# Low halves of weight pieces by accumulating DMAs in state space, attention and around the norms, with a new order in attention

## The chip, the cores and the metric

The program runs on one core of one Trainium2 chip. The metric is the device time of one execution in microseconds; the time before is the median of three runs. Engines: PE (TensorE, matmuls), DVE (VectorE), ACT (ScalarE), POOL (GpSimd) and SP (SyncE, which here issues most DMAs).

## The reference

A decoder trunk of two layers over 512 tokens of width 1024. Layer 0 mixes with a short convolution and a state space (S5), layer 1 with sparse attention: an indexer with 8 heads scores all earlier keys, the best 128 keys of each query are kept, and attention runs over those. Cut to what matters:

```python
def swiglu(x, w1, w3, w2):
    return (jax.nn.silu(x @ w1) * (x @ w3)) @ w2

def dsa_mixer(proj, cos_a, sin_a, cos_i, sin_i):      # layer 1
    q, k, v, qi, ki, wi = jnp.split(proj, C_SPLITS, axis=-1)
    ...                                                # rotary on q, k, qi, ki
        logits = jax.nn.relu(jnp.einsum('bthd,bsd->bths', qib.astype(f32), ki))
        score = jnp.einsum('bths,bth->bts', logits, wb)
        _, idx = lax.top_k(score, topk)                # topk = 128
    ...                                                # softmax(q k) v over the chosen keys

for i in range(DEPTH):                                 # DEPTH = 2
    h = layer_norm(DN_ALPHA * h + 0.5 * swiglu(h, ffn_w1[i, 0], ...), ln_g[i, 0], ln_b[i, 0])
    mix = ...                                          # layer 0: convolution and S5; layer 1: dsa_mixer
    h = layer_norm(DN_ALPHA * h + mix, ln_g[i, 1], ln_b[i, 1])
    h = layer_norm(DN_ALPHA * h + 0.5 * swiglu(h, ffn_w1[i, 1], ...), ln_g[i, 2], ln_b[i, 2])
    h = h + (p[i] @ ple_w_proj[i]) * jax.nn.sigmoid(h @ ple_w_gate[i])
```

There are six norms; below they are ln0 to ln5 in order of time.

## The kernel before

All data is f32, but a matmul takes operands of a shorter type (`fp32r`), so each operand is cut in a high part and a low part, and every product is three matmuls, high by high, high by low and low by high. The 337 blocks of weights ("pieces", 128 x 1024 f32, 512 KB each) flow through `Stream`: SP loads a piece into `wraw` (three buffers), ACT casts it to `whi` (L77), and another engine forms `wlo = wraw - whi` (L78). That engine is DVE, except between L970 and L1201 (most of attention), where `lo_engine` makes it POOL. Split pieces wait in a ring of `RING` = 7. `free` frees a used piece and splits the next one at this point of the program (`ahead`); `split_to(n)` sets how many pieces may stand split and not yet freed.

The order of instructions on every engine is that of the Python code (`manual_schedule`), so a cut stands in ACT's, DVE's or POOL's queue where `free`, `take` or `split_to` is called. Small work beside the matmuls is placed by a clock that counts matmul time (`tick`, `at`).

The stages: feed forward (L376), `tail` (L426), mixer, `tail`, feed forward, `tail`, `embed` (L1220), twice. `tail` is the end of a product with the norm woven into it: its last four pieces are multiplied for one quarter of the tokens after another, and each quarter is transposed, normalized and transposed back meanwhile. At its start the ring is filled to seven (the four pieces of the tail and three of the next stage); when three quarters of the tokens are through, `split_to(6)` splits one more, the fourth piece of the next stage. What follows a tail is a `group` (L284): four pieces, output columns in two halves of 256 tokens; in the first half (`h=0`) it needs all four pieces within 32 matmuls of 120 ns. At `h=1` it splits further ahead. After ln2 and ln5 `embed` follows instead.

The state space (`mixer_ab`, L730) is written as a row of `states(f)` and `output(f)` of four groups of channels, with products for the convolution (`hc`, `gc`, `gb`) between them. In one such round PE makes D from the inputs, DVE runs a scan (L796 to L816: `m`, `zz`, `hz`), and PE turns `hz` to outputs. `vv` is the gated convolution (L849 to L858), `L319` casts it to its high part `xh`, and the output product of L260 takes `xh`.

Attention (`mixer_dsa`, L939) makes index queries `qi` (four tiles), then the index key `ki`, with a rotary turn of each (`turn`: four DVE or POOL instructions), values `vs` (`values_in`), index weights `wi` (`weights_in`), and for each of the query tiles 1 to 3 scores: `index(i)` is eight index heads, each a matmul (L991), a relu on ACT (L994) and a multiply-add on DVE into `bias` (L996, L998). `choose(n, tiles)` runs n rounds of top-8 search on DVE (L1008 MAX8, L1010 MATCH_REPLACE8); a tile needs 16 rounds or fewer beyond the diagonal, here 16 for each of the tiles 1 to 3. Rounds that are left run inside the attention `step`s (`last_rounds`), and `chosen(i)` (L1062) turns what was found into a mask. A `step` is scores (L1102), a masked copy with maximum (L1105), an exponential (L1107), `normal` (L1109, scaling by L1114), a turn of the weights and the product with the values; heads of q and pieces of the output product (`project`) fill PE meanwhile.

Of the kernel before, what the change touches and what calls it, by code (L numbers as in the profile page):

```python
# [16 lines left out]
P = 128  # L17
T = 512
# [34 lines left out]
class Stream:  # L53
# [5 lines left out]
    def __init__(self, nc, ctx, tc, pieces):  # L59
        self.nc, self.pieces, self.n = nc, pieces, len(pieces)  # L60
        self.raw_pool = ctx.enter_context(tc.tile_pool(name="wraw", bufs=3))
        self.pool = ctx.enter_context(tc.tile_pool(name="wsplit", bufs=self.RING))
        self.raw, self.got = {}, {}
        self.loaded = self.split = self.used = self.freed = 0
        self.lo_engine = nc.vector

# [8 lines left out]

    def cut(self, t, hi, lo):
        self.nc.scalar.copy(hi, t)  # L77
        self.lo_engine.tensor_sub(lo, t, hi.bitcast(F))  # L78

    def _split(self):  # L80
        i = self.split
        while self.loaded <= i:
            self._load()
        self.got[i] = self.parts()
        self.cut(self.raw.pop(i), *self.got[i])
        self.split += 1
# [113 lines left out]
class Program:  # L200
# [73 lines left out]

    def whole(self):

        w = self.ws.take()
        b = self.bank("U")
        self.mm(b, w, self.x, range(KD), range(KD), slice(0, T))
        self.ws.free()  # L280
        self.lows()
        return b

    def group(self, done):  # L284
# [4 lines left out]
        for h in range(2):  # L289
            cols = slice(h * HALF, (h + 1) * HALF)  # L290
            if h:
                self.flush()
                ws.split_to(ws.RING - 1)
            for k0 in range(0, KD, 4):
                for m in range(0, 4, 2):
# [130 lines left out]
    def tail(self, g, g0, ln):  # L426
# [3 lines left out]
        w = [ws.take() for _ in range(4)]  # L430

        ws.split_to(ws.RING)
        ws.SPLIT = 4
# [296 lines left out]
    def mixer_ab(self, ln):  # L730
# [49 lines left out]
        self.group(have_u)  # L780
        self.pending = False

        def states(f):
# [143 lines left out]

    def turn(self, x, adder=None):

        nc = self.nc  # L930
        sin, cos = self.rope[1]
        sh = self.work.tile([P, 2, T], F, name="sh", tag="t4")
        nc.vector.stream_shuffle(sh[:, 0], x, [r ^ 8 if r < 16 else r for r in range(32)])
        nc.vector.tensor_mul(sh[:, 0], sh[:, 0], sin)
        adder = adder or nc.gpsimd
        adder.tensor_mul(sh[:, 1], x, cos)
        adder.tensor_add(x, sh[:, 0], sh[:, 1])

    def mixer_dsa(self, ln):  # L939
# [16 lines left out]

        def have(dst, b):
            nc.scalar.copy(dst, b)
            self.turn(dst)

        self.group(lambda m, b: [have(qi[:, m + i], b[i]) for i in range(2)])
        self.pending = False

        b = self.whole()
        for i in range(2):
            nc.scalar.copy(ki[64 * i:64 * i + 64], b[:64])
        wt = self.work.tile([8, T], F, name="wt", tag="t4")
        nc.scalar.activation(wt, b[64:72], AF.Copy, scale=WI_SCALE)
        self.turn(ki, v)
        ws.lo_engine = nc.gpsimd  # L970

# [11 lines left out]

        def index(i):

            n = (i + 1) * P
            sc = bias[i]
            for h in range(8):
# [8 lines left out]
                else:  # L997
                    v.scalar_tensor_tensor(sc, r[:, :n], wi[:, i, h:h + 1], sc, op0=OP.mult, op1=OP.add)  # L998
            nc.gpsimd.affine_select(sc[:, i * P:], sc[:, i * P:], pattern=[[-1, P]], compare_op=OP.is_ge,
                                    fill=NEG, base=0, channel_multiplier=1)  # L1000
# [46 lines left out]
        weights_in()  # L1047
        index(1)
        choose(6, (1,))
        values_in((2, 3))  # L1050
        ws.free(2)
        index(2)
        choose(2, (1, 2))
        run(head(k[:, 0], 0, "k"))
        index(3)
        choose(2, (1, 2))
        run(head(k[:, 1], 1, "k"))
        turn_heads([k[:, g] for g in range(2)], "k")
        choose(2, (1, 2))

        def chosen(i):
            v.tensor_scalar(bias[i], bias[i], -3.2e38, FAR, op0=OP.is_gt, op1=OP.mult)  # L1062

        for h, more in enumerate(((2, (1, 2)), (2, (1, 2)), (3, (2, 3)), (2, (2, 3)))):
            run(head(q[:, h], h, 0))
# [43 lines left out]
        def normal(i, g, r0):  # L1109
            pt, _, s = pr[i, g]  # L1110
            v.reciprocal(s[:, r0:r0 + 2], s[:, r0:r0 + 2])
            for r in (r0, r0 + 1):
                x = pt[:, r, :(i + 1) * P]
                v.tensor_scalar(x, x, s[:, r:r + 1], None, op0=OP.mult)  # L1114

# [64 lines left out]
        def last_rounds():  # L1180
            for i in range(11):
                choose(1, (3,) if i else (2, 3))
                if i in (0, 10):
                    chosen(3 if i else 2)
                yield
# [4 lines left out]
        filler = project(0)  # L1190
        step((2, 0), (1, 0), (0, 0, 0, 0, 3), (0, 0, 0, 0, 1), turn=True)
        step((0, 1), (2, 0), (2, 2, 0, 2, 3), (0, 1, 1, 0, 0))
        step((1, 1), (0, 1), (4, 2, 2, 1, 2), (0, 1, 0, 0, 0))
        step((2, 1), (1, 1), (1, 3, 1, 0, 0), (0, 1, 0, 0, 0))
# [4 lines left out]
        for _ in filler:  # L1199
            pass  # L1200
        ws.lo_engine = v  # L1201
        self.tail(O, 4, ln)
# [17 lines left out]
    def embed(self, last):  # L1220
# [12 lines left out]
        self.pending = False  # L1233
        ws.split_to(ws.RING - 1)
        new = None if last else self.pair()
        banks = self.first_two(4)
# [87 lines left out]
def pieces_dsa(w_in, w_out):  # L1324
# [3 lines left out]
    key[:, :72] = w_in[:, 2048:2120]  # L1328
    out = tiles_of(w_in[:, 1536:2048]) + tiles_of(key)
    out += [rows(w_in[:512, 1280:1536]), rows(w_in[512:, 1280:1536])]  # L1330
# [92 lines left out]
```

## Time and profile before

| | |
|---|---|
| time of 3 runs | 2010.99 us median, 2009.34 to 2012.37 |
| profiled execution | 2008.82 us, span 2006.5 us |
| PE | 1974.8 us busy, 98% of the span |
| DVE | 1048.9 us, 52% |
| ACT | 664.7 us, 33% |
| POOL | 113.6 us, 6% |
| DMA | 202.18 MB, mean 101 GB/s |

Rows of groups read: line, engine, operation, output and inputs by the program's names, count, then busy time and mean ns of one, then idle time of the engine before them and what ended it. Rows of the chain of waits: engine and line that waited, what released it, then us in all, how often, the longest or mean. Rows of the timeline: start in us, duration, engine, line, operation, and in brackets the idle time before it with its releaser. Stages of before by the timeline, in us: state space about 400 to 530, ln1's tail to 565 and then the group behind it, ln2 and embed about 944, attention about 1357 to 1550.

### The profile page before, as it was taken

Reading aid. Unit: us, or ns where it says so; the run is one execution under the profiler, and the core shown is the slowest. Engines: PE = TensorE matmul, PEld = TensorE weight load, DVE = VectorE, ACT = ScalarE, POOL = GpSimd, SP = SyncE. Lnnn points to the kernel's source line nnn. Section 1 sums busy time; section 2 is a strip of 40 time slices with the busy share of each in tenths; the row PEclk is TensorE's granted clock in tenths of the full one; section 3 lists DMA queues with packets and bytes.
Section 4 is the critical chain, followed back from the end, with each engine's and each line's share of the span. In section 5 each row is a group of like instructions: output and inputs, shape, how many; then the busy total and the mean of one; then the engine's idle time right before and its main releaser. Section 6 shows DMA issues by size and latency. Waiting matters only on the chain.

```text
span 2006.5 us, 23925 instructions
## 1 busy us (share of the span) xinstructions
PE 1974.8 (98%) x9550; PEld 1641.5 (82%) x9550; DVE 1048.9 (52%) x1959; ACT 664.7 (33%) x966; POOL 113.6 (6%) x120
## 2 busy tenths in 40 slices
PE   9999999998999999999999999998999999999999
PEld 7888888887798888888888888888776988888877
DVE  6457554667563333336555554357985643333363
ACT  5223333423353122225332222234443532222242
POOL 0001110011000000000000000002432000000000
PEclk9999999999999999999999999998999999999999
DMA  6333333344323232322332322312211142323312
GB/s 213 104 106 137 124 126 119 137 152 156 103 83 107 87 112 84 105 85 67 107 115 88 112 92 88 105 63 84 85 43 57 53 133 85 105 89 102 104 43 74
DMA packets 60559, 202.18 MB, mean 101 GB/s; under 512 B 7232, under 2 KB 11616, under 8 KB 59936
## 3 DMA queue, kind: packets, MB, share of 16 engines
q1 hardware_dynamic: 51840, 184.07, 27.8%
q0 software_dynamic: 4240, 14.44, 2.1%
q10 hardware_dynamic: 4368, 2.15, 0.4%
q8 instruction: 75, 1.23, 0.2%
q14 instruction: 36, 0.29, 0.0%
HBM read 189.10 MB, written 11.53 MB: 100 GB/s over the span
## 4 chain that ended last, share of the span: by engine, by line
PE 68%; DVE 3%; ACT 2%; issue 1%; POOL 0%; ACTq 0%; DVEq 0%; POOLq 0%
PE U L260 45%; PE D L260 14%; PE U L443 3%; PE D L443 2%; PE D L1133 1%; PE L L180 1%; PE U L1102 1%; PE U L143 0%; ACT whi L77 0%; PE D L143 0%; DVE pt L1114 0%; DVE wlo L78 0%; PE D L991 0%; PE U L273 0%; PE L L1124 0%
## 5 line engine op out<-in xcount | busy, mean ns | idle before, releaser
L260 PE MATMUL U<-xh,whi 128*128 128x512 f32 (+1 forms) x2000 | 749.0, 375 | 1.3 <-ACT xh L1139 1.0
L260 PE MATMUL U<-xl,whi 128*128 128x512 f32 (+1 forms) x2000 | 743.1, 372 | 2.1 <-DVE xl L1140 1.2
L260 PE MATMUL U<-xh,wlo 128*128 128x512 f32 (+1 forms) x2000 | 742.6, 371 | 0.0
L78 DVE TENSOR_TENSOR wlo<-wraw,whi 128x1024 fp32r<-128x1024 f32 (+1 forms) x321 | 393.8, 1232 | 307.8 <-ACT whi L77 306.9
L77 ACT CAST whi<-wraw 128x1024 fp32r<-128x1024 f32 (+1 forms) x337 | 350.5, 1045 | 550.4 <-PE D L260 295.9
L260 PEld LDWEIGHTS U<-xh,whi 128*128 128x128 f32 x2000 | 376.7, 188 | 71.2 <-ACT xh L1139 2.5
L260 PEld LDWEIGHTS U<-xl,whi 128*128 128x128 f32 x2000 | 376.7, 188 | 69.9 <-DVE xl L326 2.3
L260 PEld LDWEIGHTS U<-xh,wlo 128*128 128x128 f32 x2000 | 376.6, 188 | 64.5
L260 PE MATMUL D<-xh,whi 128*128 128x512 f32 x608 | 238.6, 392 | 8.2 <-ACT xh L319 7.7
L260 PE MATMUL D<-xl,whi 128*128 128x512 f32 x608 | 237.5, 391 | 0.0
L260 PE MATMUL D<-xh,wlo 128*128 128x512 f32 x608 | 237.2, 390 | 0.0
L373 DVE SCALAR_TENSOR_TENSOR gt<-gt,U 128x512 f32<-128x512 f32 x88 | 60.5, 687 | 264.5 <-PE U L260 208.3
L319 ACT CAST xh<-gt 128x512 fp32r<-128x512 f32 x88 | 54.6, 620 | 387.4 <-DVE gt L373 387.4
L260 PEld LDWEIGHTS D<-xh,whi 128*128 128x128 f32 x608 | 114.6, 188 | 34.6 <-ACT xh L319 8.1
L260 PEld LDWEIGHTS D<-xl,whi 128*128 128x128 f32 x608 | 114.6, 188 | 23.9 <-DVE xl L326 0.4
L260 PEld LDWEIGHTS D<-xh,wlo 128*128 128x128 f32 x608 | 114.6, 188 | 23.9
L424 DVE TENSOR_TENSOR u<-u,D 128x512 f32<-128x512 f32 x64 | 43.9, 687 | 112.7 <-PE D L260 112.7
L422 DVE SCALAR_TENSOR_TENSOR u<-u,D 128x512 f32<-128x512 f32 x40 | 27.4, 687 | 111.1 <-PE D L260 111.1
L326 DVE TENSOR_TENSOR xl<-gt,xh 128x512 fp32r<-128x512 f32 x88 | 60.3, 685 | 8.2 <-ACT xh L319 8.2
L372 ACT ACTIVATE gt<-U 128x512 f32<-128x512 f32 x88 | 52.0, 591 | 17.6 <-PE U L260 17.6
L186 DVE TENSOR_SCALAR u<-L,lnw 128x128 f32<-128x128 f32 x96 | 32.7, 403 | 26.0 <-PE L L180 26.0
L78 POOL TENSOR_TENSOR wlo<-wraw,whi 128x1024 fp32r<-128x1024 f32 x16 | 38.3, 2404 | 68.3 <-PE U L260 44.6
(318 smaller groups left out, 1553.3 us busy)
## 6 DMA issues: line engine op xcount, KB each, us to landing
wraw<-wts SPq DMA_DIRECT2D x333, 512.0 KB, 3.5
s5d<-big POOLq DMA_DIRECT2D x20, 256.0 KB, 5.1
u<-x SPq DMA_DIRECT2D x8, 256.0 KB, 5.5
s5d<-big POOLq DMA_DIRECT2D x4, 512.0 KB, 3.4
pin<-s5d SPq DMA_DIRECT2D x2, 1024.0 KB, 8.8
pin<-s5d POOLq DMA_DIRECT2D x2, 1024.0 KB, 5.3
out<-u SPq DMA_DIRECT2D x7, 256.0 KB, 2.0
pout<-s5d SPq DMA_DIRECT2D x2, 768.0 KB, 10.2
```

Of the source, the lines that this page charges most:

```text
L77: self.nc.scalar.copy(hi, t)
L78: self.lo_engine.tensor_sub(lo, t, hi.bitcast(F))
L180: p.nc.tensor.transpose(b[:, j * P:(j + 1) * P], self.z[:, c, j * P:(j + 1) * P], p.ident)
L186: p.nc.vector.tensor_scalar(out, x, gam, bet, op0=OP.mult, op1=OP.add)
L260: self.nc.tensor.matmul(out, lhsT=p[:, s], rhs=q[:, xk, cols], start=first and i == 0 and j == 0, stop=last and i == n - 1 and j == 2)
L319: self.nc.scalar.copy(hi[:, j, :], src)
L326: self.nc.vector.tensor_sub(out, src, hi)
L372: nc.scalar.activation(t[:, 0], pa, AF.Silu)
L373: nc.vector.scalar_tensor_tensor(t[:, 1], t[:, 0], 0.5, pb, op0=OP.mult, op1=OP.mult)
L422: self.nc.vector.scalar_tensor_tensor(u, u, ALPHA, d, op0=OP.mult, op1=OP.add)
L424: self.nc.vector.tensor_add(u, u, d)
L443: self.nc.tensor.matmul(b, lhsT=x, rhs=y, start=False, stop=k == TAIL - 1 and j == 2)
```

## The change

1. `cut` has a second way. When `by_dma` is set, ACT casts the high part as before (L79 after), ACT then writes the negative of the same rounded value into `wlo` (L81), and POOL issues a DMA that reads the piece from device memory a second time and adds it to `wlo` in place (L82). Else DVE subtracts as before (L84). `lo_engine` and its use of POOL are gone.
2. `by_dma` is set at the start of every `tail`, after the first `group` of the state space and after the first `group` of attention; it is cleared at `h=1` of the next `group` and in `embed`. 63 of the 337 pieces go this way: 28 around the six norms (4, 4, 6, 4, 4, 6), 35 within state space and attention. 47 DVE and 16 POOL subtractions go; 63 ACT multiplications and 63 POOL DMAs of 512 KB come.
3. Attention: the key's piece goes first; `turn` is all on DVE (two of its four instructions were POOL's for the four `qi`); both pairs of values come ahead of `index(1)`; a third of a head's projection follows every second index head; rounds of `choose` move: before the steps tile 2 gets 12 instead of 15 and tile 3 gets 2 instead of 5, in the steps `last_rounds` has 14 entries instead of 11, of which four (before: one) work on both tiles.
4. `normal`'s scaling goes from DVE (L1114) to ACT (L1140), 32 instructions.

The remarks behind # on lines of the diff name the function that the line stands in.

```diff
-    def cut(self, t, hi, lo):
+    def cut(self, t, hi, lo, piece=None):
         self.nc.scalar.copy(hi, t)
-        self.lo_engine.tensor_sub(lo, t, hi.bitcast(F))
+        if self.by_dma and piece is not None:
+            self.nc.scalar.mul(lo, t, -1.0)
+            self.nc.gpsimd.dma_start(lo, piece, accum_op=OP.add)
+        else:
+            self.nc.vector.tensor_sub(lo, t, hi.bitcast(F))
...
             if h:                                   # group
                 self.flush()
                 ws.split_to(ws.RING - 1)
+                ws.by_dma = False
...
+        ws.by_dma = True                            # tail
         ws.split_to(ws.RING)
...
         self.group(have_u)                          # mixer_ab
         self.pending = False
+        ws.by_dma = True
...
-    def turn(self, x, adder=None):
+    def turn(self, x):
...
-        adder = adder or nc.gpsimd
-        adder.tensor_mul(sh[:, 1], x, cos)
-        adder.tensor_add(x, sh[:, 0], sh[:, 1])
+        nc.vector.tensor_mul(sh[:, 1], x, cos)
+        nc.vector.tensor_add(x, sh[:, 0], sh[:, 1])
...
+        self.group(first)                           # mixer_dsa; first: key, then qi 0 to 2
         self.pending = False
-        b = self.whole()
...
-        ws.lo_engine = nc.gpsimd
+        ws.by_dma = True
+        self.whole(lambda b: have(3, b))
...
+                if h % 2:                           # index(i, part)
+                    next(part)
...
         values_in((0, 1))
         weights_in()
-        index(1)
-        choose(6, (1,))
         values_in((2, 3))
         ws.free(2)
-        index(2)
+        part = head(k[:, 0], 0, "k")
+        index(1, part)
+        choose(6, (1,))
+        run(part)
+        part = head(k[:, 1], 1, "k")
+        index(2, part)
         choose(2, (1, 2))
-        run(head(k[:, 0], 0, "k"))
-        index(3)
-        choose(2, (1, 2))
-        run(head(k[:, 1], 1, "k"))
+        run(part)
+        part = head(q[:, 0], 0, 0)
+        index(3, part)
         turn_heads([k[:, g] for g in range(2)], "k")
-        choose(2, (1, 2))
+        run(part)
+        choose(4, (1, 2))
...
-        for h, more in enumerate(((2, (1, 2)), (2, (1, 2)), (3, (2, 3)), (2, (2, 3)))):
+        for h, more in enumerate(((4, (1, 2)), (1, (2, 3)), (1, (2, 3))), 1):
...
-                v.tensor_scalar(x, x, s[:, r:r + 1], None, op0=OP.mult)
+                nc.scalar.mul(x, x, s[:, r:r + 1])
...
         self.flush()                                # embed
         self.pending = False
         ws.split_to(ws.RING - 1)
+        ws.by_dma = False
```

Three places where the order of instructions moves. First DVE in the state space, from the end of one scan (`hz`) to the start of the next (`m` from D and `pin`). Before:

```order
L816 TENSOR_TENSOR hz_3050<-m_3727 128x4x128
L78 TENSOR_TENSOR wlo<-wraw,whi 128x1024
L326 TENSOR_TENSOR xl<-z,xh 128x512
L849 TENSOR_TENSOR uu<-hc,U 128x512
L853 SCALAR_TENSOR_TENSOR vv<-uu,small,vv 128x512 x2
L78 TENSOR_TENSOR wlo<-wraw,whi 128x1024
L858 TENSOR_TENSOR vv<-vv,U 128x512
L78 TENSOR_TENSOR wlo<-wraw,whi 128x1024
L326 TENSOR_TENSOR xl<-vv,xh 128x512
L796 TENSOR_TENSOR m_3873<-D,pin 128x512
```

And after:

```order
L827 TENSOR_TENSOR hz_3052<-m_3738 128x4x128
L335 TENSOR_TENSOR xl<-z,xh 128x512
L860 TENSOR_TENSOR uu<-hc,U 128x512
L864 SCALAR_TENSOR_TENSOR vv<-uu,small,vv 128x512 x2
L869 TENSOR_TENSOR vv<-vv,U 128x512
L335 TENSOR_TENSOR xl<-vv,xh 128x512
L807 TENSOR_TENSOR m_3887<-D,pin 128x512
```

The three subtractions are gone from this stretch and nothing takes their place on DVE.

Second ACT in a `tail`, around the fourth piece of the next group (`lnt` is the normalized quarter, `u` the quarter turned back). Before:

```order
L173 ACTIVATE lnt<-U,lnm,lny 128x512 x2
L77 CAST whi<-wraw 128x1024
L188 ACTIVATE u<-L,lnw 128x128 x4
L190 CAST xh<-u 128x4x128
L173 ACTIVATE lnt<-D,lnm,lny 128x512 x2
```

And after:

```order
L179 ACTIVATE lnt<-U,lnm,lny 128x512 x2
L79 CAST whi<-wraw 128x1024
L81 ACTIVATE wlo<-wraw 128x1024
L194 ACTIVATE u<-L,lnw 128x128 x4
L196 CAST xh<-u 128x4x128
L179 ACTIVATE lnt<-D,lnm,lny 128x512 x2
```

The multiplication for `wlo` stands behind the cast, ahead of the quarter that is turned back; the DMA that waits for it stands on POOL.

Third ACT ahead of the first relus of `index(1)`. Before:

```order
L968 ACTIVATE wt<-U 8x512
L982 COPY vs<-U 128x256 x2
L976 COPY wi<-L 128x32
L994 ACTIVATE relu<-D 128x256
L994 ACTIVATE relu<-L 128x256
```

And after:

```order
L1002 COPY vs<-U 128x256 x2
L79 CAST whi<-wraw 128x1024
L81 ACTIVATE wlo<-wraw 128x1024
L79 CAST whi<-wraw 128x1024
L81 ACTIVATE wlo<-wraw 128x1024
L1015 ACTIVATE relu<-D 128x256
L1015 ACTIVATE relu<-L 128x256
```

Two pieces are split between the second pair of values and the first relu, four ACT instructions where there were none.

More of the change, by code (lines that the diff above doesn't have):

```diff
@@ L64, in __init__ @@
         self.loaded = self.split = self.used = self.freed = 0
-        self.lo_engine = nc.vector
+        self.by_dma = False
     def _load(self):
@@ L84, in _split @@
         self.got[i] = self.parts()
-        self.cut(self.raw.pop(i), *self.got[i])
+        self.cut(self.raw.pop(i), *self.got[i], self.pieces[i])
         self.split += 1
@@ L273, in token_major, with whole @@
                 self.nc.tensor.matmul(out, lhsT=x, rhs=y, start=k == 0 and j == 0, stop=k == KD - 1 and j == 2)
-    def whole(self):
+    def whole(self, done=None):
         w = self.ws.take()
@@ L279, in whole @@
         self.mm(b, w, self.x, range(KD), range(KD), slice(0, T))
+        if done:
+            done(b)
         self.ws.free()
@@ L955, in mixer_dsa, with have_key, have, first @@
                                 base=0, channel_multiplier=1)
[L957 to L961, printed above, removed]
-        self.pending = False
-        b = self.whole()
[L965 to L969, printed above, removed]
-        ws.lo_engine = nc.gpsimd
+        wt = pool.tile([P, T], F, name="relu", bufs=4)[:8]
+        def have_key(b):
+            for i in range(2):
+                nc.scalar.copy(ki[64 * i:64 * i + 64], b[:64])
+            nc.scalar.activation(wt, b[64:72], AF.Copy, scale=WI_SCALE)
+            self.turn(ki)
+        def have(i, b):
+            nc.scalar.copy(qi[:, i], b)
+            self.turn(qi[:, i])
+        def first(m, b):
+            for i in range(2):
+                if m + i:
+                    have(m + i - 1, b[i])
+                else:
+                    have_key(b[i])
+        self.group(first)
+        self.pending = False
+        ws.by_dma = True
+        self.whole(lambda b: have(3, b))
         def weights_in():
@@ L982, in values_in, with index @@
                 nc.scalar.copy(vs[:, t], b[:, :256])
-        def index(i):
+        def index(i, part):
             n = (i + 1) * P
@@ L1180, in last_rounds @@
         def last_rounds():
[L1181 to L1184, printed above, removed]
+            for i in range(14):
+                choose(1, (3,) if i > 3 else (2, 3))
+                if i in (3, 13):
+                    chosen(3 if i > 3 else 2)
                 yield
@@ L1190, in mixer_dsa @@
         filler = project(0)
-        step((2, 0), (1, 0), (0, 0, 0, 0, 3), (0, 0, 0, 0, 1), turn=True)
-        step((0, 1), (2, 0), (2, 2, 0, 2, 3), (0, 1, 1, 0, 0))
-        step((1, 1), (0, 1), (4, 2, 2, 1, 2), (0, 1, 0, 0, 0))
+        step((2, 0), (1, 0), (0, 0, 0, 0, 3), (0, 1, 0, 0, 1), turn=True)
+        step((0, 1), (2, 0), (2, 2, 0, 2, 3), (0, 1, 1, 1, 0))
+        step((1, 1), (0, 1), (4, 2, 2, 1, 2), (0, 1, 0, 1, 0))
         step((2, 1), (1, 1), (1, 3, 1, 0, 0), (0, 1, 0, 0, 0))
@@ L1200, in mixer_dsa @@
             pass
-        ws.lo_engine = v
         self.tail(O, 4, ln)
@@ L1328, in pieces_dsa @@
     key[:, :72] = w_in[:, 2048:2120]
-    out = tiles_of(w_in[:, 1536:2048]) + tiles_of(key)
+    out = tiles_of(key) + tiles_of(w_in[:, 1536:2048])
     out += [rows(w_in[:512, 1280:1536]), rows(w_in[512:, 1280:1536])]
```

## The prediction

> **What bounds the kernel now.** I read the page's totals first, then the chain of waits of PE, then the windows around its gaps, then the timeline inside them.
>
> ```profile
> span 2006.5 us, 23925 instructions
> PE 1974.8 (98%) x9550; PEld 1641.5 (82%) x9550; DVE 1048.9 (52%) x1959; ACT 664.7 (33%) x966; POOL 113.6 (6%) x120
> ```
>
> PE is idle for 2006.5 - 1974.8 = 31.7 us of the span. The change takes no matmul away, so its gain is PE idle time and slow PE time. PE's waits, as engine, line, releaser, then us in all, count and longest:
>
> ```profile
> PE D L260 <- ACT xh L319: 7.7, 1, 7.7
> PE D L991 <- issue: 5.4, 1, 5.4
> PE U L260 <- ACT pp L1231: 1.7, 4, 0.6
> PE D L143 <- DVE u L422: 1.5, 1, 1.5
> ```
>
> The first lies in the state space, the second ahead of the index scores; the third is `embed`, the fourth the gates of the state space. The windows give busy us of PE, PEld, DVE, ACT and POOL, the granted clock, DMA share and GB/s:
>
> ```profile
> 490.00:540.00 50.00, 40.54 (x182) 32.66 (x181) 29.09 (x38) 17.71 (x23) 4.93 (x9) 0.93 0.33 106
> 1392.00:1425.00 33.00, 25.55 (x130) 18.41 (x129) 27.69 (x56) 14.89 (x33) 9.63 (x6) 0.84 0.26 84
> 1425.00:1460.00 35.00, 34.45 (x156) 28.46 (x154) 34.15 (x94) 16.28 (x23) 19.14 (x12) 1.00 0.26 87
> 1480.00:1500.00 20.00, 16.12 (x92) 11.85 (x92) 17.48 (x52) 8.06 (x24) 5.21 (x4) 1.00 0.07 25
> 1520.00:1548.00 28.00, 26.97 (x152) 19.07 (x151) 13.82 (x34) 11.02 (x19) 7.33 (x4) 1.00 0.12 39
> ```
>
> Granted clock below 1.00 stands only where PE had a long gap. In 1425:1460 DVE is busy 34.15 of 35 us: there DVE is the bound, and PE is kept busy by work that it would have to do anyway.
>
> **A. State space (gain).** The timeline of the last round:
>
> ```profile
> 474.31 1.95 PE L790 MATMUL D<-ut,pin 128*128 128x128 f32 x16
> 480.69 1.23 DVE L78 TENSOR_TENSOR wlo<-wraw,whi 128x1024 fp32r<-128x1024 f32 x1 [2.67 <-ACT whi L77]
> 482.44 0.68 DVE L796 TENSOR_TENSOR m<-D,pin 128x512 f32<-128x512 f32 x1
> 492.42 1.22 DVE L78 TENSOR_TENSOR wlo<-wraw,whi 128x1024 fp32r<-128x1024 f32 x1
> 497.09 1.22 DVE L78 TENSOR_TENSOR wlo<-wraw,whi 128x1024 fp32r<-128x1024 f32 x1
> 498.94 0.62 ACT L319 CAST xh<-vv 128x512 fp32r<-128x512 f32 x1 [2.40 <-DVE vv L858]
> 499.61 0.80 PE L260 MATMUL D<-xh,whi 128*128 128x512 f32 x1 [7.72 <-ACT xh L319]
> 503.76 0.40 PE L260 MATMUL D<-xh,whi 128*128 128x512 f32 x1
> 504.00 0.39 PE L260 MATMUL D<-xl,whi 128*128 128x512 f32 x1
> ```
>
> PE has D ready at 474.31 + 1.95 = 476.26, but DVE starts the scan at 482.44, behind a subtraction for which it had stood waiting on ACT's cast. Without that subtraction the scan can start 482.44 - 476.26 = 6.2 us earlier, and without the two at 492.42 and 497.09 its result comes 2.4 us earlier still: 8.6 us for `xh`. PE waited 7.72, so the wait goes nearly whole. It also cost speed: the ten matmuls from 499.61 to 503.76 took 4.15 us, at the later pitch of 504.00 - 503.76 = 0.24 they take 2.4, so 1.75 more. I take 9 of these 9.5 (low end 4, if ACT's three added multiplications hold the chain up as the casts did). Against it, the gates behind:
>
> ```profile
> 524.71 1.05 ACT L77 CAST whi<-wraw 128x1024 fp32r<-128x1024 f32 x1 [4.69 <-PE U L260]
> ```
>
> This cast stands ahead of the gates' sigmoids, for which PE waits in the end (the 1.5 on L422), and now a multiplication follows it. Before has none of this size on ACT; it reads and writes the same tiles as the cast, so I price it as the cast, 1.05 (between 0.8 and 1.3 the sum moves by 2 us, mostly in C): +1.05. Sum of A: -8.
>
> **B. Attention (gain).**
>
> ```profile
> 1400.57 0.35 DVE L996 TENSOR_SCALAR bias<-relu,wi 128x256 f32<-128x256 f32 x1 [1.74 <-ACT relu L994]
> 1409.98 1.99 ACT L77 CAST whi<-wraw 128x1024 fp32r<-128x1024 f32 x2
> 1459.75 1.17 DVE L1062 TENSOR_SCALAR bias<-bias 128x256 f32<-128x256 f32 x1
> L1008 DVE MAX8 m<-bias 128x8 f32<-128x384 f32 x16 | 8.7, 545 | 0.1
> L1010 DVE MATCH_REPLACE8 bias<-m,bias 128x384 f32<-128x384 f32 x15 | 8.1, 540 | 0.0
> L998 DVE SCALAR_TENSOR_TENSOR bias<-relu,wi,bias 128x384 f32<-128x384 f32 x7 | 6.3, 895 | 0.7
> L998 DVE SCALAR_TENSOR_TENSOR bias<-relu,wi,bias 128x512 f32<-128x512 f32 x7 | 5.3, 751 | 0.7
> L1008 DVE MAX8 m<-bias 128x8 f32<-128x512 f32 x6 | 4.0, 675 | 0.0
> L1010 DVE MATCH_REPLACE8 bias<-m,bias 128x512 f32<-128x512 f32 x5 | 3.4, 676 | 0.0
> L1114 DVE TENSOR_SCALAR pt<-pt,sm 128x128 f32<-128x128 f32 (+3 forms) x32 | 16.0, 542 | 0.6
> L78 POOL TENSOR_TENSOR wlo<-wraw,whi 128x1024 fp32r<-128x1024 f32 x16 | 38.3, 2404 | 68.3 <-PE U L260 44.6
> ```
>
> DVE's stretch from the first multiply-add to the mask of tile 1 lasts 1460.92 - 1400.57 = 60.3 us. Three rounds each of tiles 2 and 3 leave it: 3 x (0.545 + 0.540) + 3 x (0.675 + 0.676) = 7.3. An op on 384 columns that takes 895 ns where one on 512 takes 751 was held up; the subtractions on POOL (2.4 us each against 1.23 on DVE) ran beside it. At 0.6 us the seven give 2.0 back, and with the mask, 1.17 us for 256 columns, I put the whole at 3.5. So the stretch shrinks to about 49. It starts later, though: ahead of the relus stand two casts (1.99 us for the two, by the row at 1409.98) and two multiplications of the same size, 4 us in all, part of it in time that ACT had to spare; I put the first multiply-add at 1402.9, and the end at 1452, 9 earlier. The wait of 5.4 us goes, but each `index` now has a start that PE must await (some 3 us each at two of them and at the first step, where POOL adds the turned queries), so PE gains 6.5 of the 9.
>
> In the steps DVE loses 16.0 us of scaling and gets 7.3 of rounds. PE's idle time there is (20 - 16.12) + (28 - 26.97) = 4.9 us; I take 3.5, since ACT, with 32 more instructions and the multiplications, now stands in the same loop. Sum of B: -10. Ends: -2, if the four ACT instructions and the new waits take back all but 2, and -14, if both parts come whole.
>
> **C. The group behind a norm (loss).** The fourth piece behind ln1, and plain DMAs (KB each, us to landing) as nearest rows:
>
> ```profile
> 564.39 1.04 ACT L77 CAST whi<-wraw 128x1024 fp32r<-128x1024 f32 x1
> 565.47 1.23 DVE L78 TENSOR_TENSOR wlo<-wraw,whi 128x1024 fp32r<-128x1024 f32 x1 [0.64 <-ACT whi L77]
> 569.04 0.28 PE L260 MATMUL U<-xh,wlo 128*128 128x256 f32 x1
> s5d<-big POOLq DMA_DIRECT2D x4, 512.0 KB, 3.4
> pin<-s5d SPq DMA_DIRECT2D x2, 1024.0 KB, 8.8
> pin<-s5d POOLq DMA_DIRECT2D x2, 1024.0 KB, 5.3
> ```
>
> DVE had `wlo` at 566.70, 2.3 us ahead of PE's first use at 569.04. Now ACT's multiplication ends about 564.39 + 2 x 1.05 = 566.5, and only then may the DMA start; it has 2.55 us, and no plain DMA of this size lands in less than 3.4. If it takes X, PE stands for X - 2.55, behind each of ln0, ln1, ln3 and ln4, four times. No row has an accumulating DMA. It reads the piece and what stands in `wlo`, twice the bytes, so the nearest row is POOL's read of 1024 KB, 5.3 us: 4 x 2.75 = +11. Low end 3.4: +3.4. High end 8.0 (SP's 1024 KB took 8.8, part of it other traffic): +22.
> The Trainium skill (DMA: Bandwidth & Descriptors, Anatomy of one DMA) has a fit for DMAs issued by GpSimd, 2.0 us and 436 KB per us; by it I estimate 3.2 us for 512 KB, which the 3.4 agrees with, and 4.4 for twice the bytes, so +7.4 here. I stay with 5.3, which the trace has for that size. The Trainium skill (Collectives: The Full Stack, The bandwidth ceiling) holds that an add in a DMA costs by its two source reads and not by the add; no run here shows that yet.
>
> **D. `embed` (loss).**
>
> ```profile
> 944.04 1.04 ACT L77 CAST whi<-wraw 128x1024 fp32r<-128x1024 f32 x1
> 944.99 1.55 ACT L1231 COPY pp<-U 128x512 f32<-128x512 f32 x3
> ```
>
> PE waits for these copies (the row of 1.7), and a multiplication of 1.05 now comes between: twice, +2.1.
>
> **E. At nothing.** The other 55 or so pieces land several us before use, as the ring runs up to six pieces ahead; their cover goes if X reaches some 8 us or POOL's queue stops. POOL's 63 issues delay only POOL, whose 38.3 us of subtractions go. DMA share is 0.33 at most in the windows; 33 MB more on 202 leave room. The turns moved from POOL to DVE fall under the first group's matmuls.
>
> **Sum:** -8 - 10 + 11 + 2.1 = -5, on the profiled execution's 2008.82, so 2004. The median of the runs, 2010.99, is 2.2 above that execution: 2006.
>
> **Rivals.** Changes within 0.2% (4 us) count as none, about what a measurement can tell here.
> 1. The accumulating DMA is nearly as quick as a plain one, X = 3.4 to 4.3: C is +3.4 to +7, the sum about -11, 2000 us. For it: the plain rows. Against: twice the bytes.
> 2. It ends on the other side, by one mechanism: the first use of `wlo` behind a norm. With A, B and D as above the sum is zero at 4 (X - 2.55) = 16, X = 6.55, and above +4 from X = 7.55. At X = 8 with gaps of 5.5 us, PE also starts again slowly, as behind the gap of 7.72 above, 1.75 each: 4 x 7.2 - 16 = +13, 2024; without the slow starts +6, 2017. For it: 8.8 on SP for 1024 KB. Against: 5.3 and 3.4 on POOL's own queue.
> The Trainium skill (SBUF — State Buffer, SBUF: two separate sides) names a way to it: DVE in one of its faster modes keeps GpSimd from writing the descriptors of its DMAs. No row of before shows one.
> The Trainium skill (TensorE: Matmul & The Clock Gate, Part 1) has the clock fall after idle windows of some 3.4 us; the trace agrees in so far as the 7.72 and the 5.4 were followed by a clock under 1.00.
> 3. Attention keeps its time: the new start costs DVE 4 us, PE waits at each `index`, and ACT takes DVE's place in the steps. B is -2 and the sum +3: 2014, no change or slower. For it: DVE at 34.15 of 35; against: 16 + 7.3 us taken off DVE where it is the bound.
> 4. It does not do what it says: the state space keeps its wait, since ACT, with 63 more instructions of a microsecond, replaces DVE as the late engine. A is -3, the sum 0: 2011.
>
> **Chances.** Forecast 0.45, rival 1 0.2, rival 2 0.15, rival 3 0.12, rival 4 0.08. Faster by over 0.2%: most of rival 1 (0.18), 0.6 of the forecast (0.28), a little of 3 and 4 (0.03), 0.49. Slower: rival 2 (0.14) and parts of the forecast and of 3 (0.09), 0.23. Same: 0.28. The range reaches from 1997, where rival 1 meets B's high end, to 2017, where C alone goes to its high end; the forecast's own is 2000 to 2012.
>
> **What would show it.** A: no wait of PE on L319's `xh` in the state space, the next matmuls at full pitch. B: DVE's first multiply-add to the mask of tile 1 in some 49 us, steps with under 2 us of PE idle time. C: four waits of 2 to 3 us of PE, on the first product with the fourth piece's `wlo`, released by POOL's DMA queue, 5.3 us after its issue. D: the row of 1.7 grows to some 3.8. The prediction is wrong first if X is not near 5.3, each us of it being 4 us of the sum; second if ACT holds up the relus.

## The result: slower, 2033 us

The changed kernel takes 2033.33 us (median of 4 runs, 2032.37 to 2035.30), before in the same runs 2011.68 (2009.34 to 2013.09): a ratio of 1.0112, 95% interval 1.0097 to 1.0127. The forecast was 2006, and the range ended at 2017. The profiled execution took 2035.3 us with a span of 2033.5, 27.0 over the span of before. First the page of after (groups: busy us, mean ns of one; queues: packets, MB, share of 16 engines' span; issues: KB each, median us to landing):

```profile
span 2033.5 us, 24001 instructions
PE 1987.2 (98%) x9550; PEld 1648.8 (81%) x9550; DVE 975.7 (48%) x1888; ACT 739.3 (36%) x1061; POOL 116.8 (6%) x159
L81 ACT ACTIVATE wlo<-wraw 128x1024 fp32r<-128x1024 f32 x63 | 66.7, 1058 | 0.0
q1 hardware_dynamic: 51840, 184.07, 27.5%
q0 software_dynamic: 13312, 47.47, 11.0%
wlo<-wts POOLq DMA_DIRECT2D x63, 512.0 KB, 8.4
```

DVE lost 73 us and ACT gained 75, as the change says; neither decides. An accumulating DMA lands 8.4 us after its issue (the median of all 63; the four behind the norms that PE waits for took 7.5 to 7.9), where I had put 5.3. PE's waits in after:

```profile
PE U L266 <- DMA wlo<-wts: 21.5, 4, 5.6
PE D L1159 <- ACT relu L1152: 2.9, 2, 2.5
PE D L266 <- ACT xh L328: 2.8, 1, 2.8
PE D L149 <- DVE u L431: 2.4, 1, 2.4
PE U L266 <- ACT xh L1165: 2.0, 1, 2.0
PE U L266 <- ACT pp L1256: 1.7, 2, 0.8
```

The first row is new and answers to nothing in before. The 7.7 on `xh` fell to 2.8, and the 5.4 of attention is gone, but a 2.5 and a 2.0 in the steps took its place. Where the time went shows best by stage. I cut each trace at the transposes of the norms (L180 before, L186 after), which all kernels have: a "tail" runs from a norm's first transpose to its last, which stands in the first half of the group behind it, so that a wait for the fourth piece lies inside; the mixers lie between ln0's last and ln1's first, and ln3's last and ln4's first. In us, for all kernels of this study (named by their experiments below):

| kernel | ln0 tail | state space | ln1 tail | ln3 tail | attention | ln4 tail |
|---|---|---|---|---|---|---|
| before | 22.3 | 158.1 | 22.4 | 22.3 | 197.2 | 22.4 |
| after | 30.2 | 156.8 | 29.5 | 29.6 | 196.7 | 29.1 |
| 1 fourth piece on DVE | 22.3 | 154.8 | 22.3 | 22.3 | 199.3 | 22.4 |
| 2 fourth piece, no add | 26.0 | 150.2 | 24.5 | 27.0 | 197.3 | 28.3 |
| 3 load put off | 29.4 | 158.7 | 28.3 | 30.0 | 198.3 | 29.3 |
| 4 multiplied first | 28.7 | 157.2 | 27.4 | 27.9 | 196.6 | 28.1 |
| 5 two halves | 27.6 | 152.3 | 25.1 | 26.8 | 197.4 | 27.6 |
| 6 y by itself | 30.2 | 149.9 | 28.3 | 29.5 | 199.7 | 29.3 |
| 7 scaling on DVE | 30.6 | 152.4 | 29.4 | 29.1 | 195.8 | 29.4 |
| 8 the three edits | 22.3 | 150.6 | 22.3 | 22.4 | 196.1 | 22.3 |
| 9 state space on DVE | 22.3 | 163.1 | 22.3 | 22.3 | 196.0 | 22.4 |
| 10 attention on DVE | 22.3 | 149.9 | 22.4 | 22.3 | 205.3 | 22.3 |
| 11 old order of attention | 22.3 | 148.1 | 22.3 | 22.3 | 199.4 | 22.3 |
| 12 mixers only | 22.3 | 148.1 | 22.3 | 22.3 | 196.1 | 22.4 |

After against before: the four tails +29.0, the state space -1.3, attention -0.5, and the rest of the program -0.2, together 27.0, the difference of the spans. The medians differ by less, 21.7: the profiled execution of after is the slowest of its four, and that of before is 2.9 us below its median here. So the split holds for these two executions. Nor does a stage take the same time in each execution: in the seven kernels of the table that share after's code of attention (after and 1 to 6), attention takes 196.6 to 199.7.

**The tails.** Timeline of after behind ln1:

```profile
571.35 1.04 ACT L79 CAST whi<-wraw 128x1024 fp32r<-128x1024 f32 x1
572.29 1.06 ACT L81 ACTIVATE wlo<-wraw 128x1024 fp32r<-128x1024 f32 x1
573.73 0.85 POOL L82 DMA_DIRECT2D wlo<-wts  x1 [26.42 <-DVE lny L166]
575.87 0.28 PE L266 MATMUL U<-xl,whi 128*128 128x256 f32 x1
581.71 0.58 PE L266 MATMUL U<-xh,wlo 128*128 128x256 f32 x1 [5.56 <-DMA wlo<-wts]
582.09 0.42 PE L266 MATMUL U<-xh,whi 128*128 128x256 f32 x1
```

The multiplication ends at 573.35, POOL issues at 573.73, and PE goes on at 581.71, 8.4 us behind the multiplication, having waited 5.56. Then it runs slowly: matmuls of 256 columns take 0.42 us and not 0.28. So each tail costs some 5.4 us of wait and about 2 of slow restart (PE running slowly when it goes on).

**The state space.** DVE is early now, as forecast, and stops inside the scan:

```profile
484.20 0.69 DVE L807 TENSOR_TENSOR m<-D,pin 128x512 f32<-128x512 f32 x1 [1.26 <-PE D L801]
490.31 0.69 DVE L810 TENSOR_TENSOR m<-D,pin 128x512 f32<-128x512 f32 x1 [3.80 <-DMA turn<-y]
502.82 0.62 ACT L328 CAST xh<-vv 128x512 fp32r<-128x512 f32 x1 [0.50 <-DVE vv L869]
503.49 0.79 PE L266 MATMUL D<-xh,whi 128*128 128x512 f32 x1 [2.80 <-ACT xh L328]
```

DVE waits for PE (1.26) and not PE for DVE, until L810: `m` takes the buffer that held `y` (both stand under the tag t4, which has two), and `y` is still being read by the DMA that stores it. This store got slow because the accumulating DMAs fill the DMA engines; in experiment 9, which takes them out of the state space, its median is 2.6 us again. Issues of `y`, first before, then after:

```profile
turn<-y ACTq DMA_DIRECT2D x4, 256.0 KB, 2.7
```

```profile
turn<-y ACTq DMA_DIRECT2D x4, 256.0 KB, 7.8
```

and a window of the state space, before and then after (busy us of PE, PEld, DVE, ACT, POOL, clock, DMA share, GB/s):

```profile
432.00:461.00 29.00, 29.00 (x158) 25.05 (x157) 21.44 (x35) 10.37 (x13) 0.55 (x1) 1.00 0.49 169
```

```profile
440.00:470.00 30.00, 30.00 (x163) 25.86 (x162) 18.71 (x33) 13.44 (x16) 5.27 (x8) 1.00 0.86 250
```

**Attention.** DVE's stretch, and one place in the steps:

```profile
1424.19 0.35 DVE L1017 TENSOR_SCALAR bias<-relu,wi 128x256 f32<-128x256 f32 x1 [5.79 <-ACT relu L1015]
1474.00 0.70 DVE L1088 TENSOR_SCALAR bias<-bias 128x256 f32<-128x256 f32 x1
1495.47 1.03 ACT L79 CAST whi<-wraw 128x1024 fp32r<-128x1024 f32 x1
1496.41 1.05 ACT L81 ACTIVATE wlo<-wraw 128x1024 fp32r<-128x1024 f32 x1
1499.77 0.56 ACT L1152 COPY relu<-L 128x512 f32<-128x512 f32 x1
1500.38 1.13 PE L1159 MATMUL D<-relu,vs 128*128 128x512 f32 x2 [2.49 <-ACT relu L1152]
```

The stretch lasts 1474.70 - 1424.19 = 50.5 us (60.3 before). But in the steps ACT works without a pause from 1494.66 to 1501.4, and PE stands for its copy.

### The profile page after: what moved, and what is told of

The parts are those of the page before. It is cut to its first block, busy times and chain, and to the rows that moved or that the text cites. A ratio compares the mean times of both kernels' runs of the same rounds, so it can differ in the third digit from the quotient of the medians.

```text
span 2033.5 us, 24001 instructions
## 1 busy us (share of the span) xinstructions
PE 1987.2 (98%) x9550; PEld 1648.8 (81%) x9550; DVE 975.7 (48%) x1888; ACT 739.3 (36%) x1061; POOL 116.8 (6%) x159
## 3 DMA queue, kind: packets, MB, share of 16 engines
q1 hardware_dynamic: 51840, 184.07, 27.5%
q0 software_dynamic: 13312, 47.47, 11.0%
q8 instruction: 75, 1.23, 0.2%
## 4 chain that ended last, share of the span: by engine, by line
PE 89%; DVE 3%; ACT 3%; DMA 3%; issue 2%; SPq 0%; POOL 0%; DVEq 0%; ACTq 0%; POOLq 0%
PE U L266 59%; PE D L266 20%; PE U L453 3%; PE D L453 3%; DMA wlo<-wts 2%; DMA turn<-y 1%; PE L L186 1%; PE D L1159 1%; PE U L279 1%; PE U L1128 0%; PE D L1012 0%; PE D L149 0%; PE U L149 0%; DVE zz L816 0%; ACT pt L1140 0%
## 5 line engine op out<-in xcount | busy, mean ns | idle before, releaser
L266 PE MATMUL U<-xh,wlo 128*128 128x512 f32 (+1 forms) x2000 | 747.0, 373 | 21.5 <-DMA wlo<-wts 21.5
L79 ACT CAST whi<-wraw 128x1024 fp32r<-128x1024 f32 (+1 forms) x337 | 351.2, 1045 | 550.5 <-PE D L266 295.8
L84 DVE TENSOR_TENSOR wlo<-wraw,whi 128x1024 fp32r<-128x1024 f32 (+1 forms) x274 | 332.0, 1215 | 311.3 <-ACT whi L79 309.4
L266 PEld LDWEIGHTS U<-xh,wlo 128*128 128x128 f32 x2000 | 380.2, 190 | 87.1 <-DMA wlo<-wts 22.4
L82 POOL DMA_DIRECT2D wlo<-wts x63 | 55.2, 886 | 1463.8 <-DVE wlo L84 1042.0
L431 DVE SCALAR_TENSOR_TENSOR u<-u,D 128x512 f32<-128x512 f32 x40 | 27.4, 686 | 114.6 <-PE D L266 114.6
L81 ACT ACTIVATE wlo<-wraw 128x1024 fp32r<-128x1024 f32 x63 | 66.7, 1058 | 0.0
```

The source lines that it names most:

```text
L81: self.nc.scalar.mul(lo, t, -1.0)
L82: self.nc.gpsimd.dma_start(lo, piece, accum_op=OP.add)
L84: self.nc.vector.tensor_sub(lo, t, hi.bitcast(F))
L266: self.nc.tensor.matmul(out, lhsT=p[:, s], rhs=q[:, xk, cols], start=first and i == 0 and j == 0, stop=last and i == n - 1 and j == 2)
L431: self.nc.vector.scalar_tensor_tensor(u, u, ALPHA, d, op0=OP.mult, op1=OP.add)
```

## The experiments

Times are medians; a ratio is against before in the same runs (2009.4 to 2011.7). Edits are against the changed kernel unless said.

**1. The fourth piece on DVE.**

```diff
+                        ws.by_dma = False
                         ws.split_to(6)
+                        ws.by_dma = True
```

> The changed kernel, but the fourth piece behind each norm gets its low part from DVE again; the other 57 pieces stay with the DMA. Theory: the accumulating DMA of that one piece makes PE wait 5.4 us behind ln0, ln1, ln3 and ln4, and a slow restart follows each (1.5 to 2.6 us), 29 us by stage lengths; so 2033.3 - 29 = 2004 (2001 to 2008), no wait of PE on wlo. Rival: the load on the DMA engines and on ACT is spread over all 63 pieces, and the fourth piece only shows it; then another wait takes its place and the time is over 2015.

2006.40 us, ratio 0.9978 (0.9969 to 0.9986). All four tails are back at 22.3. Of 63 DMAs the six of the fourth pieces, four of them behind ln0, ln1, ln3 and ln4, make the kernel slower; PE's longest row is now one of `embed`:

```profile
PE U L266 <- ACT pp L1258: 3.7, 4, 1.6
```

**2. The same DMA without the add.**

```diff
-            self.nc.gpsimd.dma_start(lo, piece, accum_op=OP.add)
+            if self.plain:                # set around the tail's split_to(6)
+                self.nc.gpsimd.dma_start(lo, piece)
+            else:
+                self.nc.gpsimd.dma_start(lo, piece, accum_op=OP.add)
```

> The changed kernel, but POOL's DMA of the fourth piece behind each norm overwrites wlo and does not add (those six low parts then hold the whole piece, so the output differs). If the add with its second read is what takes long, the DMA lands like a plain one of 512 KB, 3.4 to 4 us after its issue, PE waits 1 to 1.5 us, four times, without slow restarts: 2033 - 29 + 5 = 2009 (2007 to 2013). If it is POOL's path or the load of the next piece beside it, the waits stay over 4 us and the time stays over 2025.

2017.71 us, ratio 1.0043 (1.0027 to 1.0059): between the two theories.

```profile
PE U L269 <- DMA wlo<-wts: 11.3, 4, 4.3
```

The waits are 2.0, 2.1, 2.9 and 4.3 us, half of 21.5. The tails together fall by 12.6 us (118.4 to 105.8), less than half of the 29.0 that the change added to them; most of the rest of the gain in time is the state space, 150.2 in this execution without an edit there. What the add costs shows on POOL's queue q0 behind ln3, where nothing else is on it (packets, MB, share of 16 engines). After, in the window of 12 us from 1370, and then this run, in the one of 11 us from 1355:

```profile
q0 software_dynamic: 144, 0.52, 28.0%
```

```profile
q0 software_dynamic: 144, 0.52, 13.7%
```

A packet took an engine 0.280 x 12 x 16 / 144 = 0.37 us with the add and 0.137 x 11 x 16 / 144 = 0.17 without. So about half of the wait is the add's. Without it the DMA, which still turns f32 into the matmul's type, landed 4.4 to 6.6 us after its issue at these four places. That is slower than the 3.4 that the prediction took for a plain DMA of this size, but the row of 3.4 is a store: `s5d` lies in device memory. POOL's plain reads of 512 KB stand in another row of before:

```profile
pt<-p POOLq DMA_DIRECT2D x2, 512.0 KB, 4.5
```

They took 3.8 and 5.3 us. So most of the second half is what such a read takes without any add. Whether the change of type comes on top, and what made it 6.6 behind ln4, is not settled.

**3. The load beside it put off.**

```diff
-                        ws.split_to(6)
+                        ws.SPLIT, ws.MORE = 6, 0      # ahead() loads up to freed + SPLIT + MORE;
+                        ws.ahead()                    # the next split_to sets MORE to 2 again
```

> The changed kernel, but SP's load of the next piece, which in the changed kernel starts within 1 us of the accumulating DMA of the fourth piece behind a norm, is put off to the second half of the group. Theory: the two share the DMA engines, and alone the accumulating DMA lands 1.3 to 2 us sooner: the four waits fall from 5.4 to about 3.7 us, 2033 - 7 = 2026. Rival: the time is its own (start, two reads and a write), waits stay within 0.7 us of 5.4 and the time within 2 us of 2033.

2036.01 us, ratio 1.0130 (1.0117 to 1.0144).

```profile
PE U L267 <- DMA wlo<-wts: 19.1, 4, 5.2
```

The edit did not do what I meant, so this run does not test the load. In its trace SP's loads start at 386.26, 574.32, 1371.37 and 1599.69, 0.02 us behind the end of the multiplication, as in after (386.38, 573.38, 1371.60 and 1598.01, some 0.03 behind). SP runs ahead of the other engines, so wherever the Python code issues this load, it waits for the `wraw` buffer alone, which the multiplication frees. The 19.1 in place of 21.5 is then no effect of the load: the kernels of 6 and 7, with after's code in the tails, have 20.3 and 20.4. What the trace of after does show is that the load lands 1.2 to 1.5 us after the adding DMA's first packet, and the adding DMA itself 4.0 to 4.4 us later still. The load overlaps the smaller part of it; what it costs is not measured.

**4. Multiplied first, cast second** (for the fourth piece).

```diff
+        if self.by_dma and piece is not None and self.first:
+            self.nc.scalar.mul(lo, t, -1.0)
+            self.nc.gpsimd.dma_start(lo, piece, accum_op=OP.add)
+            self.nc.scalar.copy(hi, t)
+            return
```

> The changed kernel, but ACT multiplies first and casts second for the fourth piece behind a norm. whi is then 1.05 us later, which PE has to spare there, and the DMA starts 1.05 us sooner. If PE waits on the chain multiplication, DMA, wlo, each of the four waits falls by 1.05 us, 5.4 to 4.3: 2033 - 4 = 2029 (2028 to 2030.5). Rival: the DMA's end is set by other traffic (the next piece's load) and waits stay: 2033.

2027.74 us, ratio 1.0084 (1.0071 to 1.0096).

```profile
PE U L271 <- DMA wlo<-wts: 15.7, 4, 4.2
```

The waits fell by 1.45 each (1.05 expected), the tails by 1.0 to 2.1. PE's wait hangs on the chain of multiplication, DMA and `wlo`, and starting the DMA sooner took time off it.

**5. Two halves** (for the fourth piece).

```diff
+            for c in (slice(0, WIDE // 2), slice(WIDE // 2, WIDE)) if self.first else (slice(0, WIDE),):
+                self.nc.gpsimd.dma_start(lo[:, c], piece[:, c], accum_op=OP.add)
```

> The changed kernel, but the accumulating DMA of the fourth piece behind a norm is issued as two DMAs of 256 KB, in the order in which PE uses the halves. If the landing grows with bytes (8 us for 512 KB, of which some 2.2 us pass before the first packet), the first half lands at about 5 us, PE waits 2.5 to 3.5 us for it instead of 5.4, and the second is hidden or costs a short second wait: 2033 - 9 = 2024 (2020 to 2029). Rival: the time is one of start and end alone, the first half lands as late as the whole: 2033 or more.

2020.36 us, ratio 1.0053 (1.0039 to 1.0067).

```profile
PE U L267 <- DMA wlo<-wts: 12.6, 4, 3.6
wlo<-wts POOLq DMA_DIRECT2D x12, 256.0 KB, 5.9
```

The waits are 2.6 to 3.6 us, and there is one at each place. The landing grows with the bytes: at these four places the first halves landed 4.9 to 5.9 us after their issue, the whole pieces of after 7.5 to 7.9 (the 5.9 of the row is the median of first and second halves). The tails fall by 11.3 us together.

**6. y in a buffer of its own.**

```diff
-            y = self.work.tile([P, 4, P], F, name="y", tag="t4")
+            y = pool.tile([P, 4, P], F, name="y")
```

> The changed kernel, but y of the state space's output has a buffer of its own. In the changed kernel DVE stands 3.8 us in the last scan (L810) until the DMA that stores y has landed, since m takes y's buffer; PE then waits 2.8 us on xh and starts again slowly. Theory: with a buffer of its own the scan does not stop, xh comes 3.8 us earlier, and wait and slow restart go: -4 to -6 us, 2028 (2026 to 2030). Rival: the outputs z, whose DMAs are late as well, or ACT's multiplications hold PE at the same place: within 1.5 us of 2033.

2030.24 us, ratio 1.0099 (1.0086 to 1.0112), 3 us below after, at the edge of what can be told. The stage tells more: the state space takes 149.9 us in place of 156.8, and the wait of 2.8 is no longer among PE's waits; attention, whose code is the same, took 3 us more in this execution. Among the kernels with the DMAs in the state space, those with the shared buffer show 150.2 to 158.7 and those with y by itself 148.1 to 150.6: the shared buffer makes the stage hang on when one store lands.

**7. The scaling on DVE.**

```diff
-                nc.scalar.mul(x, x, s[:, r:r + 1])
+                v.tensor_scalar(x, x, s[:, r:r + 1], None, op0=OP.mult)
```

> The changed kernel, but the scaling of the softmax weights is on DVE again. The steps of attention took 90.1 us from first score to last product with values, 86.0 before. Theory: ACT is the late engine in the steps of the changed kernel (PE waits 2.5 us on a copy that stands behind a cast and a multiplication, and 2.0 on a cast of the output), so without the 32 scalings on ACT the steps shorten by 2 to 4 us: 2030.5 (2029 to 2032). Rival: DVE becomes late again by the 16 us it gets back: 2033 to 2037.

2029.26 us, ratio 1.0100 (1.0086 to 1.0115), 4 below after by the medians and 2.4 by the ratios, whose intervals overlap.

```profile
PE D L1159 <- ACT relu L1152: 0.9, 2, 0.5
```

The 2.5 us behind ACT's copy are gone. That the time met my range is in part luck: by stages this execution gains 4.4 us in the state space, where nothing was edited, and 0.9 in attention. Attention takes 195.8 to 196.1 in the kernels with scaling on DVE and the new order (7, 8, 9, 12), and 196.6 to 199.7 in the seven with scaling on ACT, so some gain is there, smaller than the 2 to 4 us that I expected in the steps, which take 89.1 in place of 90.1.

**8. The three edits** of 1, 6 and 7 at once.

> The changed kernel with three edits at once: the fourth piece behind a norm on DVE, y in a buffer of its own, the softmax scaling on DVE. If the three losses lie in different stages they add: 27 less by the first (measured alone: 2006.4 against 2009.8 of before), some 3 to 5 by the second, 4 by the third, so 1999 (1997 to 2002), 0.995 of before. Rival: they share a cause (ACT too full, DMA engines too full), one repairs the other, and the time is 2003 or more.

1999.45 us, ratio 0.9948 (0.9935 to 0.9960). The times add: alone the edits gave 26.9, 3.1 and 4.1, together 33.9. By stages, against after, the tails give 29.1, the state space 6.2 and attention 0.6, and `embed` takes 2.4 back (D below). The first two are losses of their own, in stages of their own; the third is hardly larger than what attention differs by between executions.

**9. State space on DVE** (against 8).

```diff
         self.group(have_u)
         self.pending = False
-        ws.by_dma = True
```

> The kernel with the three edits, but the low parts inside the state space on DVE as well. It prices what the DMAs do there once y has its own buffer: if DVE's subtractions were what made PE wait 7.7 us for xh, that wait and its slow restart return, +6 to +9 over the kernel with the three edits, 2006. Rival: taking them off DVE brings nothing, since the DMA engines or ACT delay other things by as much: within 2 us of it.

2009.84 us, ratio 1.0001 (0.9992 to 1.0010), 10.4 above 8, a little more than expected. The wait of before is back:

```profile
PE D L266 <- ACT xh L328: 8.6, 1, 8.6
```

**10. Attention on DVE** (against 8).

```diff
-        ws.by_dma = True
         self.whole(lambda b: have(3, b))
```

> The kernel with the three edits, but the low parts inside attention on DVE as well. If DVE is the bound ahead of the steps (27.78 busy of 29 us there in the changed kernel), some eight subtractions of 1.23 us make the steps start later: +3 to +8 over the kernel with the three edits, 2004. Rival: ACT, rid of as many multiplications of 1.05 us in front of relus and copies, gains as much: within 2 us, or faster.

2010.74 us, ratio 1.0006 (0.9997 to 1.0015), 11.3 above 8, more than the 3 to 8 expected. PE waits at the first step for queries that POOL adds only once DVE is done:

```profile
PE U L1129 <- POOL q L1067: 7.6, 2, 7.0
```

The new order leans on DVE having no weights to split. The new order with POOL's subtractions was not run.

**11. The old order of attention.** Before, with `cut` of the changed kernel, by DMA within the state space and attention, y by itself:

```diff
-        ws.lo_engine = nc.gpsimd
+        ws.by_dma = True
```

> The kernel before with its own order of attention, but POOL's subtractions in attention and DVE's in the state space replaced by multiplication and accumulating DMA, y in its own buffer; norms and gates as before. The state space gives -8 (150 us in place of 158 by stage). In attention (197.2 us from ln3's last transposes to ln4's first in before, 196.7 in the changed kernel, 196.1 with scaling on DVE): if the DMAs bring the gain and the new order takes it back, the stage is 192 or less and the time 1996 or less; if the DMAs bring little there and the order carries what there is, it stays at 196 to 199, time 2001 to 2004.

2002.01 us, ratio 0.9957 (0.9944 to 0.9969). All of it is the state space (148.1). Attention takes 199.4, 2.2 more than with POOL's subtractions:

```profile
PE D L997 <- issue: 4.8, 1, 4.8
PE D L997 <- ACT relu L1000: 3.1, 1, 3.1
```

From ln3's last transposes the first score comes at 96.7 us (before 94.0, after 89.4, 12 at 90.9), and the steps take 85.4 (before 86.0, after 90.1, 12 at 88.0). So the new order brings the steps forward by 6 us and gives 2.6 back in them, in single executions: the four kernels with the new order and the scaling on DVE differ by 1.4 in the steps (88.0 to 89.4).

**12. Mixers only.** 8, but pieces around norms and behind the convolution are DVE's:

```diff
-        ws.by_dma = True                  # tail
+        ws.by_dma = False
         ws.split_to(ws.RING)
...
         self.lows()                       # mixer_ab, behind the convolution
+        ws.by_dma = False
         for j in range(KD):
```

> The new order of attention, the DMAs only within the state space (up to its convolution's end) and attention; all pieces around norms and at the gates on DVE, y in its own buffer, scaling on DVE. Against the kernel with the three edits (1999.45) it takes the multiplications away from the copies that embed waits for and from the gates: embed loses 2.4 us of PE time twice there and 1.4 before, the gates 4.2 and 2.3 before, so -2 - 2 = 1996 (1994 to 1998). Rival: the other norm pieces on DVE delay the norms or the feed forward, or nothing changes: 1999 or more.

1997.00 us, ratio 0.9933 (0.9919 to 0.9946): the fastest kernel here by its median, ahead of before and after; its interval and that of 8 overlap.

```profile
PE U L266 <- ACT pp L1257: 1.7, 4, 0.6
PE D L149 <- DVE u L431: 1.5, 1, 1.5
```

Both waits stand where before has them (1.7 and 1.5), against 3.6 and 2.4 in 8.

## Why the prediction was wrong

**C, the groups behind norms: +11 forecast, +29 measured; this alone puts the time out of range.** Place, count and chain were right: four waits, on the first use of the fourth piece's `wlo`. The step that failed is the price of each wait, and two terms of it were mis-sized. X, put at 5.3 from POOL's read of 1024 KB with a high end of 8.0, was 8.0 to 8.4 from the end of the multiplication to PE's start: four waits of 5.2 to 5.6, 21.5 in all. And the slow restart, which I put at nothing in C and kept for rival 2, follows every one of these waits: (29.0 - 21.5) / 4 = 1.9 us each. The nearest row was the wrong one: it had twice the bytes, but it did not add. The low end was wrong as well: 3.4 is a store, and POOL's plain reads of 512 KB took 3.8 and 5.3 (2). Experiment 2 prices the add at about half of the waits. The page's rows give a like price over the whole program: queue q0 went from

```profile
q0 software_dynamic: 4240, 14.44, 2.1%
```

to 13312 packets at 11.0%, so (0.110 x 2033.5 - 0.021 x 2006.5) x 16 / 9072 = 0.32 us of an engine for each packet, against 0.275 x 2033.5 x 16 / 51840 = 0.17 on the queue of plain loads. Rival 2, with a chance of 0.15, is what happened; its 2024 took A and B for granted.

The Trainium skill (TensorE: Matmul & The Clock Gate, Part 1) puts the slow state behind an idle window of some 3.4 us, by a window that runs freely. The trace agrees for 5.4 us; shorter gaps went both ways: the 2.80 at 503.49 was followed by matmuls of 0.79 us, twice their usual time, and of the gaps of 2.0 and 2.1 in experiment 2, the second was followed by matmuls at full speed, the first (ln0) by full speed for 0.9 us and then by matmuls of 256 columns at 0.41 us for some 3.

**A, the state space: -8 forecast, -1.3 measured.** The mechanism was right: DVE's subtractions made `xh` late; 9 shows the wait come back, 6 and 8 show -7.5 to -8.2 once y is by itself, 11 and 12, which also leave the gates to DVE, -10. The step that failed is in E, "DMA share is 0.33 at most in the windows; 33 MB more on 202 leave room". I averaged over the program and took windows behind the scan; in the state space the share was 0.49, rose to 0.86, and slowed a store that I had not looked at, on whose buffer the scan depends.

**B, attention: -10 forecast, -0.5 measured.** The first part held in kind: the stretch shrank to 50.5 us (49 forecast) and started 2.5 us later against the norm before it (1400.57 - 1363.19 = 37.4 and 1424.19 - 1384.29 = 39.9; 2.3 forecast); the steps began 4.6 us earlier (6.5 forecast). The second part had the wrong sign: the steps were 4.1 us longer, not 3.5 shorter. I counted PE's idle time there as DVE's doing. With the DMAs the steps take 85.4 in the old order (11), 88.0 in the new (12), and 90.1 with the scaling on ACT as well (after): some 2.6 for the new order, with the moved rounds in it, and some 2 for ACT, which became late as rival 3 says. Single executions differ by 1 to 2 us there, so these are sizes, not exact prices; that attention gained nothing near 10 is clear, whether it gained 0.5 is not. And the DMAs as such bring attention's old order nothing against POOL (11); that POOL's subtractions, slow as they were, stayed out of ACT's way is my reading of PE's wait on ACT's relu there (3.1 us, 1.3 in before).

**D, `embed`: +2.1 forecast, nothing measured.** The waits on `pp` are 1.7 us as before, two of 0.8 in place of four. In 8, with the fourth piece on DVE, the forecast loss of about 1 us each does appear (3.6 in place of 1.7), and in 12 it goes. The timelines of ln2's last quarter show what I left out. Before, then after:

```profile
938.13 1.45 ACT L173 ACTIVATE lnt<-D,lnm,lny 128x512 f32<-128x512 f32 x2 [2.38 <-DVE lnm L170]
939.34 1.03 PE L180 MATMUL L<-ident,lnt 128*128 128x128 f32 x8
```

```profile
951.02 1.45 ACT L179 ACTIVATE lnt<-D,lnm,lny 128x512 f32<-128x512 f32 x2 [0.20 <-DVE lnm L176]
953.46 1.03 PE L186 MATMUL L<-ident,lnt 128*128 128x128 f32 x8
```

In before DVE splits the fourth piece (1.23 us) ahead of this quarter's moments, and ACT waits for them. In after that subtraction is gone: ACT starts 2.44 us ahead of PE's transposes instead of 1.21, which makes up for the multiplication of 1.05 that comes later. In 8 the subtraction is back on DVE (ACT waits 2.40, and starts 1.22 ahead), the multiplication stays, and the loss shows.

## What to carry to other kernels

A DMA that adds takes work off DVE and costs the DMA engines about twice the time of a plain one for each packet: price it by a run of its own, and use it only where its result is needed far later than it is issued; the four pieces here with 2.5 us to spare cost more than all others gained. Before reading a run, look in its trace whether the edit moved what it was meant to move: experiment 3 did not. When transfers are added, look at the DMA share of the stage where they go, and at every buffer that waits for a store in that stage. When work moves from one late engine to another, read what that other engine does between two things that PE waits for, and not its share of the span.

## What the runs showed of the hardware

A packet of an adding DMA took a DMA engine 0.37 us behind ln3, one of the same DMA without the add 0.17. Behind the norms an adding DMA of 512 KB landed in 7.5 to 7.9 us (the median of all 63 is 8.4), the first of two halves of 256 KB in 4.9 to 5.9, the same 512 KB without the add in 4.4 to 6.6; a plain read of 512 KB took 3.8 and 5.3 on POOL's queue, 3.5 (median) on SP's. With the DMA share of a stage at 0.86, a store of 256 KB by another queue went from 2.7 to 7.8 us. PE fell to about half speed behind a gap of 2.8 us and, after 0.9 us at full speed, behind one of 2.0; behind one of 2.1 it did not.
